# One PSUM bank for three value products and the softmax denominators in a fused attention layer

## The chip, the cores and the metric

The kernel runs on one core of a Trainium2 chip. The metric is the device time of one execution in microseconds (us). A core has a matrix engine (TensorE, in the profile PE for its matrix products and PEld for its weight loads), a vector engine (DVE), a scalar engine for functions and copies (ACT), GpSimd (POOL), and a queue engine that issues transfers (SP). TensorE writes to PSUM alone, which here is used as eight banks of 128 partitions by 512 fp32 numbers.

## The reference

Two layers over 2048 tokens of width 1024. Layer 0 is a gated linear recurrence with a pooling mixer; the change does not touch its arithmetic. Layer 1 is attention with 16 heads of 64 numbers and a cumulative forget bias, cut here to what matters:

```python
q, k, v, g, fl = jnp.split(h @ w_in, ...)
cumf = jnp.cumsum(jax.nn.log_sigmoid(fl + b_f), axis=1)
for blk in range(SEQ // 128):
    logits = q[blk] @ k[:q1].T * scale + cumf[blk][:, None] - cumf[None, :q1]
    probs = softmax(where(mask, logits, -inf), axis=-1)   # exp(...) / sum of exp(...)
    outs.append(probs @ v[:q1])
o = concatenate(outs) * silu(g)
x = x + gate * (o @ w_out)
```

Scores, softmax and values are fp32 in the reference. The kernel keeps that precision by splitting an operand into two parts, `hi` (rounded to the matrix engine's fp32r form) and `lo` (what the rounding left), and adding the products of hi with hi, hi with lo and lo with hi.

## The kernel before

Tokens are worked on in four segments of 512. For each segment layer 0 runs, then layer 1. In layer 1 a head `h` of segment `s` attends to `4*(s+1)` key blocks of 128 keys: those of older segments come back from memory (`K1o`, `K2o`, `Vo`), and the last four are the segment's own (`K1`, `K2`, `Vc`). An own block `b` needs only the queries from `128*b` on, so those four blocks work on 512, 384, 256 and 128 queries. Over the whole program there are 640 key blocks: 448 of 512 queries, and 64 each of 384, 256 and 128.

`attend` (L1116) works on one key block as follows. Two products put the scores, keys by queries, into a bank `pst` (tag `st`, two banks); a block on the diagonal gets a mask by a third. ACT takes the exponential twice, once rounded into `ph` (L1153) and once in place (L1154), and DVE subtracts the two into `pl` (L1156), which ends the bank's use. `values` (L1129) runs two blocks later (`LAG = 2`). It multiplies `ph` with 128 columns that hold the low and the high half of the values, into bank `pov` (tag `o`, one bank, 64 partitions for each half), and `pl` with 66 columns, the high half and two columns of ones, into bank `pol` (tag `o2`, one bank). The sum of `ph` over keys is not taken by TensorE: GpSimd adds every block's `ph` into the tile `la` (L1160 to L1164), 128 partitions by 512, and the sum over the partitions is taken later.

At a head's end ACT copies one half of `pov` (L1175), DVE adds the ones row of `pol` to `la` (L1176) and joins the three parts of the result (L1177, L1178); `la` is then split (L1180, L1181). After every second head, `finish` (L1184) sums `la` over the partitions by four products into `pL`, takes the reciprocal by a logarithm and an exponential, and scales the pair of heads.

While head `h` runs, `max_pass` (L1091) takes the row maxima of head `h+1` in banks `pmx` (DVE reduces them, L1102 and L1104), and writes them, transposed as `pmt`, by an ACT copy into a row of the second query tile (L1114). The second score product of the next head's first block reads that row. `quad_attention` (L1207) steps `attend` and `max_pass` together, and `weave` (L216) deals out between the key blocks the products of projections that later work needs (`pqk`, `pv`, `pgt`, `py`). The tile framework then sets the final order on each engine by its own scheduling, with priorities from the order of the code; each engine works through its list in that order.

Projection weights arrive as `raw`; ACT rounds them (`wt`, L295), and DVE and GpSimd share the subtraction for the low part (L184 by way of L296).

PSUM's eight banks are: `pj` two (projections), `st` two (scores), `o` one, `o2` one, `mx` two (maxima, transposes, `pL`). In layer 0 `o2` also holds one quarter of the output projection (L830).

Of the kernel before, what the change touches and what calls it, by code (L numbers as in the profile page):

```python
# [18 lines left out]
P = 128  # L19
# [16 lines left out]
def trunk(ctx, tc, x, cvec, norm_g, ada_c, ada_w, ada_b, ada_bg, lbp, w0, w0o, w1, w1f, w1o,  # L36
# [31 lines left out]
    def tmp(name, dt=F32, shape=(P, 512)):  # L68
        return tp.tile(list(shape), dt, name=name, tag="tmp")
# [7 lines left out]
    def ps_st(name):  # L77
        return ps.tile([P, 512], F32, name=name, tag="st", bufs=2)

    def ps_o(name):  # L80
        return ps.tile([P, 512], F32, name=name, tag="o", bufs=1)

    def ps_o2(name):
        return ps.tile([P, 512], F32, name=name, tag="o2", bufs=1)

# [3 lines left out]
    def f(ap):  # L89
        return ap.bitcast(F32)  # L90
# [23 lines left out]

    pairr = cp.tile([P, 3 * HD], F32R, name="pairr")
    of = tmp("of")[:, 0:3 * HD]
    V.memset(of, 0.0)
    V.memset(of[:, HD:2 * HD], 1.0)
    V.tensor_copy(pairr, of)

# [699 lines left out]
    def out_first(s):  # L820

        L = seg0[s]
        xs = L["x"] = []
        for tb in range(NTB):
            xt = xp.tile([P, D], F32, name="xo", tag="xs")
            nc.sync.dma_start(xt, x[s * SEG + tb * P:s * SEG + (tb + 1) * P, :])
            xs.append((xt, once([P, 4], f"ss{tb}")))
        wt = next_w(("b", 0))

        L["py"] = wt, [(ps_pj, ps_pj, ps_o2, ps_mx)[tb]("py")[:, 0:256] for tb in range(NTB)]  # L830
        for tb in range(NTB):
            assert L["cores"] >= 3
            proj_N(L["py"][1][tb], wt, L["mix"], tb, (4, 5, 6, 7, 0, 1, 2), last=False)
            yield
# [281 lines left out]
    def attend(s, h):  # L1116
# [5 lines left out]
        vc = L["v", pair]  # L1122
        la = kp.tile([P, SEG], F32, name="la", tag="la", bufs=1)
        po, pol = ps_o("pov"), ps_o2("pol")
        nkb = NTB * (s + 1)
# [3 lines left out]
        def values(b, q0, kb, vv, ph, pl):  # L1129
            end = kb == nkb - 1  # L1130
            mm(po[:, q0:], vv[:, b, 0:P], ph[:, q0:], start=(kb == 0), stop=end)
            mm(pol[0:HD + 2, q0:], vv[:, b, HD:], pl[:, q0:],
               start=(kb == 0), stop=end)

        for c in range(s + 1):
# [8 lines left out]
            for b in range(NTB):  # L1144
# [11 lines left out]
                split_lo(pl[:, q0:], st[:, q0:], ph[:, q0:])  # L1156
                if kb == 0:
                    first = f(ph)
                    if s == 0:
                        G.tensor_copy(la, first)  # L1160
                elif kb == 1 and s > 0:
                    G.tensor_tensor(la, first, f(ph), op=ALU.add)
                else:
                    G.tensor_tensor(la[:, q0:], la[:, q0:], f(ph[:, q0:]), op=ALU.add)  # L1164
                todo.append((b, q0, kb, vv, ph, pl))
# [6 lines left out]
        if j == 0:  # L1172
            L["u", pair] = xp.tile([P, 2, SEG], F32, name="u", tag="xs")
        u = L["u", pair][j * HD:(j + 1) * HD, 0, :]
        S.copy(u, po[HD:P])  # L1175
        V.tensor_tensor(la[0:1], pol[HD:HD + 1], la[0:1], op=ALU.add)  # L1176
        V.tensor_tensor(u, po[0:HD], u, op=ALU.add)  # L1177
        V.tensor_tensor(u, pol[0:HD], u, op=ALU.add)  # L1178
        lh, ll = tmp("lh", F32R), tmp("ll", F32R)
        S.copy(lh, la)  # L1180
        split_lo(ll, la, lh)  # L1181
        L["l", h] = (lh, ll)

    def finish(s, h):  # L1184
# [6 lines left out]
        pL = ps_misc("pL")  # L1191
        for i in range(2):
            for part in range(2):
                mm(pL, pairr[:, (1 - i) * HD:(1 - i) * HD + P], L["l", h - 1 + i][part], start=(i + part == 0), stop=(i + part == 2))
        S.activation(rl, pL, AF.Ln)
# [192 lines left out]
```

## Time and profile before

| | |
|---|---|
| median of 3 runs | 3030.41 us (3029.74 to 3030.75) |
| the profiled execution's own time | 3029.48 us |
| its span, first to last instruction | 3027.8 us |
| mean granted TensorE clock | 0.975 of 2.4 GHz |
| PE busy | 2808.9 us, 93% of the span, 17212 products |
| DVE busy | 2301.3 us, 76% |
| ACT busy | 1826.4 us, 60% |
| POOL busy | 1172.5 us, 39% |

Busy time is the union of an engine's instructions. Products follow one another before the one ahead has ended, and their ends are modelled by the profiler, so PE can show as busy through a short wait; the distance from one start to the next tells what a product costs. The attention of the four segments lies at 382 to 697, 979 to 1388, 1672 to 2164 and 2452 to 3005 us; layer 0 lies between them.

### The profile page before, as it was taken

Reading aid. Unit: us, or ns where it says so; the run is one execution under the profiler, and the core shown is the slowest. Engines: PE = TensorE matmul, PEld = TensorE weight load, DVE = VectorE, ACT = ScalarE, POOL = GpSimd, SP = SyncE. Lnnn points to the kernel's source line nnn. Section 1 sums busy time; section 2 is a strip of 40 time slices with the busy share of each in tenths; the row PEclk is TensorE's granted clock in tenths of the full one; section 3 lists DMA queues with packets and bytes.
Section 4 is the critical chain, followed back from the end, with each engine's and each line's share of the span. In section 5 each row is a group of like instructions: output and inputs, shape, how many; then the busy total and the mean of one; then the engine's idle time right before and its main releaser. Section 6 shows DMA issues by size and latency. Waiting matters only on the chain.

```text
span 3027.8 us, 49244 instructions
## 1 busy us (share of the span) xinstructions
PE 2808.9 (93%) x17212; PEld 2390.2 (79%) x17212; DVE 2301.3 (76%) x4390; ACT 1826.4 (60%) x3743; POOL 1172.5 (39%) x992
## 2 busy tenths in 40 slices
PE   4699999989999999989999999998999999999998
PEld 3688887879888887868878887776898877777777
DVE  8667678776676788886586788889667678888886
ACT  3344566774445666775455676768635467777774
POOL 3111233323211444444212355554432136566665
PEclk9899999999999999999999999999999999999999
DMA  7523365534233444533333443553342334333442
GB/s 246 174 57 102 106 141 139 119 91 124 79 102 110 119 119 104 131 99 115 100 95 116 122 124 115 126 133 113 97 126 71 114 104 115 105 113 107 113 138 86
DMA packets 207888, 348.97 MB, mean 115 GB/s; under 512 B 24068, under 2 KB 70788, under 8 KB 205080
## 3 DMA queue, kind: packets, MB, share of 16 engines
q1 hardware_dynamic: 201816, 329.03, 39.0%
q10 hardware_dynamic: 5824, 16.79, 1.7%
q8 instruction: 137, 2.24, 0.3%
q14 instruction: 111, 0.91, 0.1%
HBM read 293.58 MB, written 52.14 MB: 114 GB/s over the span
## 4 chain that ended last, share of the span: by engine, by line
PE 60%; DVE 19%; ACT 11%; DMA 4%; issue 4%; POOL 1%; SPq 0%; ACTq 0%; DVEq 0%; POOLq 0%
PE py L42 10%; PE pgt L42 8%; PE pqk L42 8%; PE pst L42 6%; PE pv L42 6%; PE pmx L42 4%; PE pov L42 3%; PE pol L42 3%; PE pf L42 3%; PE pq L42 3%; PE pl L42 3%; DVE pl L184 2%; DVE wt L184 2%; ACT wt L295 1%; DMA raw<-in_w_dram 1%
## 5 line engine op out<-in xcount | busy, mean ns | idle before, releaser
L184 POOL TENSOR_TENSOR wt<-raw,wt 128x512 fp32r<-128x512 f32 x287 | 419.5, 1470 | 1030.9 <-ACT wt L295 975.1
L1164 POOL TENSOR_TENSOR la<-la,ph 128x512 f32<-128x512 f32 (+3 forms) x528 | 610.6, 1156 | 385.7 <-ACT ph L1153 342.9
L184 DVE TENSOR_TENSOR pl<-pst,ph 128x512 fp32r<-128x512 f32 (+3 forms) x640 | 386.9, 605 | 133.4 <-ACT pst L1154 102.2
L1153 ACT ACTIVATE ph<-pst 128x512 fp32r<-128x512 f32 (+3 forms) x640 | 340.6, 532 | 235.1 <-PE pst L42 224.9
L42 PE MATMUL pqk<-wt,h 128*128 128x256 f32 x3072 | 433.1, 286 | 5.5 <-DVE h L497 2.7
L42 PEld LDWEIGHTS pqk<-wt,h 128*128 128x128 f32 x3072 | 411.9, 192 | 25.2 <-DVE h L497 3.5
L42 PE MATMUL pgt<-h,wt 128*128 128x512 f32 x1536 | 403.9, 405 | 0.0
L295 ACT CAST wt<-raw 128x512 fp32r<-128x512 f32 x578 | 335.2, 621 | 74.9 <-PE py L42 33.3
L42 PE MATMUL pv<-wt,h 128*128 128x256 f32 x2304 | 345.0, 298 | 10.7 <-DVE h L184 6.6
L42 PEld LDWEIGHTS pv<-wt,h 128*128 128x128 f32 x2304 | 326.1, 204 | 28.9 <-DVE h L184 9.6
L42 PEld LDWEIGHTS pgt<-h,wt 128*128 128x128 f32 x1536 | 293.1, 194 | 63.2 <-issue 1.9
L1154 ACT ACTIVATE pst<-pst 128x512 f32<-128x512 f32 (+3 forms) x640 | 340.0, 531 | 0.0
L184 DVE TENSOR_TENSOR wt<-raw,wt 128x512 fp32r<-128x512 f32 x291 | 265.7, 918 | 73.4 <-ACT wt L295 71.9
L1102 DVE TENSOR_REDUCE mxs<-pmx 128x1 f32<-128x512 f32 x384 | 258.6, 684 | 20.3 <-PE pmx L42 17.2
L42 PE MATMUL py<-wt,o 128*128 128x256 f32 x1536 | 202.2, 286 | 1.4 <-ACT o L1200 1.2
L42 PE MATMUL py<-wt,mix 128*128 128x256 f32 x1536 | 198.2, 287 | 2.3 <-DVE yt L844 2.1
L42 PEld LDWEIGHTS py<-wt,o 128*128 128x128 f32 x1536 | 192.8, 192 | 6.7 <-ACT o L1200 1.5
L42 PEld LDWEIGHTS py<-wt,mix 128*128 128x128 f32 x1536 | 187.9, 191 | 9.8 <-issue 4.5
L42 PE MATMUL pst<-Q,K1o 128*128 128x512 f32 x384 | 162.6, 424 | 23.2 <-DVE pl L184 21.7
L42 PE MATMUL pmx<-K2o,Q 67*128 67x512 f32 x384 | 162.0, 426 | 21.9 <-ACT Q L1077 10.2
L42 PE MATMUL pov<-ph,Vo 128*128 128x512 f32 x384 | 162.8, 425 | 6.6 <-ACT ph L1153 6.2
L1104 DVE CUSTOM_DVE_ANT_0 pmx<-pmx,mq 128x128 f32<-128x128 f32 (+3 forms) x256 | 124.6, 497 | 55.6 <-PE pmx L42 53.8
(251 smaller groups left out, 5309.1 us busy)
## 6 DMA issues: line engine op xcount, KB each, us to landing
raw<-in_w_dram SPq DMA_DIRECT2D x448, 256.0 KB, 3.5
K2o<-k2d SPq DMA_DIRECT2D x192, 160.0 KB, 3.4
Vo<-vd SPq DMA_DIRECT2D x96, 260.0 KB, 2.7
K1o<-k1d SPq DMA_DIRECT2D x96, 256.0 KB, 3.4
raw<-in_w1o_dram SPq DMA_DIRECT2D x66, 256.0 KB, 3.6
raw<-in_w0o_dram SPq DMA_DIRECT2D x64, 256.0 KB, 3.2
vd<-Vc SPq DMA_DIRECT2D x48, 260.0 KB, 8.1
ada<-in_ada_w_dram ACTq DMA_DIRECT2D x12, 1024.0 KB, 5.0
```

The costliest lines, as they stand in the source:

```text
L42: return nc.tensor.matmul(*a, **k)
L184: (eng or V).tensor_tensor(out_t, full, f(hi), op=ALU.subtract)
L295: S.copy(wt[:, 0, sl, :], raw)
L1102: V.tensor_reduce(mxs[:, i, c:c + 1], pm[:, 0:n], axis=AX.X, op=ALU.max)
L1104: V.tensor_tensor_reduce(pm[:, 0:n], pm[:, 0:n], mq[:, SEG - n:], 1.0, NEG, op0=ALU.add, op1=ALU.max, accum_out=mxs[:, i, c:c + 1])
L1153: S.activation(ph[:, q0:], st[:, q0:], AF.Exp)
L1154: S.activation(st[:, q0:], st[:, q0:], AF.Exp)
L1164: G.tensor_tensor(la[:, q0:], la[:, q0:], f(ph[:, q0:]), op=ALU.add)
```

## The change

The three partial products of a key block all go into the one bank `pov`, one after the other: `ph` with the 66 columns of high values and ones (64 value rows and the rows of ones), `ph` with the 64 columns of low values, `pl` with the 66 columns. Row 64 of the bank then holds the whole denominator. GpSimd's sum `la` and the bank `pol` go. The bank set free is given to the scores, which now have three. At a head's end ACT rounds row 64 into a row of a new constant tile `sums` (zero elsewhere), copies the 64 result rows to `u`, and DVE writes the low part of the denominator 32 partitions further. `finish` then needs one product over 97 partitions in place of four over 128. The quarter of the output projection that was in `o2` takes a score bank.

```diff
@@ -75,13 +75,10 @@
         return ps.tile([P, 512], F32, name=name, tag="pj", bufs=2)
 
     def ps_st(name):
-        return ps.tile([P, 512], F32, name=name, tag="st", bufs=2)
+        return ps.tile([P, 512], F32, name=name, tag="st", bufs=3)
 
     def ps_o(name):
         return ps.tile([P, 512], F32, name=name, tag="o", bufs=1)
-
-    def ps_o2(name):
-        return ps.tile([P, 512], F32, name=name, tag="o2", bufs=1)
 
     def ps_mx(name):
         return ps.tile([P, 512], F32, name=name, tag="mx", bufs=2)
@@ -112,11 +109,15 @@
     eps1 = cp.tile([P, 1], F32, name="eps1")
     V.memset(eps1, EPS)
 
-    pairr = cp.tile([P, 3 * HD], F32R, name="pairr")
-    of = tmp("of")[:, 0:3 * HD]
+    pairr = cp.tile([P, P], F32R, name="pairr")
+    of = tmp("of")
     V.memset(of, 0.0)
-    V.memset(of[:, HD:2 * HD], 1.0)
-    V.tensor_copy(pairr, of)
+
+    sums = cp.tile([P, SEG], F32R, name="sums")
+    V.tensor_copy(sums, of)
+    V.memset(of[0:HD, 0:HD], 1.0)
+    V.memset(of[HD:P, HD:P], 1.0)
+    V.tensor_copy(pairr, of[:, 0:P])
 
     NL = 7
     lmask = cp.tile([P, NL, P // 2], U8, name="lmask")
@@ -827,7 +828,7 @@
             xs.append((xt, once([P, 4], f"ss{tb}")))
         wt = next_w(("b", 0))
 
-        L["py"] = wt, [(ps_pj, ps_pj, ps_o2, ps_mx)[tb]("py")[:, 0:256] for tb in range(NTB)]
+        L["py"] = wt, [(ps_pj, ps_pj, ps_st, ps_mx)[tb]("py")[:, 0:256] for tb in range(NTB)]
         for tb in range(NTB):
             assert L["cores"] >= 3
             proj_N(L["py"][1][tb], wt, L["mix"], tb, (4, 5, 6, 7, 0, 1, 2), last=False)
@@ -1120,17 +1121,16 @@
         Q1, Q3, K1, K2 = L["ops", h]
         pair, j = h // 2, h % 2
         vc = L["v", pair]
-        la = kp.tile([P, SEG], F32, name="la", tag="la", bufs=1)
-        po, pol = ps_o("pov"), ps_o2("pol")
+        po = ps_o("pov")
         nkb = NTB * (s + 1)
         kb = 0
         todo = []
 
         def values(b, q0, kb, vv, ph, pl):
             end = kb == nkb - 1
-            mm(po[:, q0:], vv[:, b, 0:P], ph[:, q0:], start=(kb == 0), stop=end)
-            mm(pol[0:HD + 2, q0:], vv[:, b, HD:], pl[:, q0:],
-               start=(kb == 0), stop=end)
+            mm(po[0:HD + 2, q0:], vv[:, b, HD:], ph[:, q0:], start=(kb == 0), stop=False)
+            mm(po[0:HD, q0:], vv[:, b, 0:HD], ph[:, q0:], start=False, stop=False)
+            mm(po[0:HD + 2, q0:], vv[:, b, HD:], pl[:, q0:], start=False, stop=end)
 
         for c in range(s + 1):
             if c < s:
@@ -1154,14 +1154,6 @@
                 S.activation(st[:, q0:], st[:, q0:], AF.Exp)
                 pl = tmp("pl", F32R)
                 split_lo(pl[:, q0:], st[:, q0:], ph[:, q0:])
-                if kb == 0:
-                    first = f(ph)
-                    if s == 0:
-                        G.tensor_copy(la, first)
-                elif kb == 1 and s > 0:
-                    G.tensor_tensor(la, first, f(ph), op=ALU.add)
-                else:
-                    G.tensor_tensor(la[:, q0:], la[:, q0:], f(ph[:, q0:]), op=ALU.add)
                 todo.append((b, q0, kb, vv, ph, pl))
                 if len(todo) > LAG:
                     values(*todo.pop(0))
@@ -1171,15 +1163,11 @@
             values(*t)
         if j == 0:
             L["u", pair] = xp.tile([P, 2, SEG], F32, name="u", tag="xs")
-        u = L["u", pair][j * HD:(j + 1) * HD, 0, :]
-        S.copy(u, po[HD:P])
-        V.tensor_tensor(la[0:1], pol[HD:HD + 1], la[0:1], op=ALU.add)
-        V.tensor_tensor(u, po[0:HD], u, op=ALU.add)
-        V.tensor_tensor(u, pol[0:HD], u, op=ALU.add)
-        lh, ll = tmp("lh", F32R), tmp("ll", F32R)
-        S.copy(lh, la)
-        split_lo(ll, la, lh)
-        L["l", h] = (lh, ll)
+        r = j * HD
+        hi = sums[r:r + 1]
+        S.copy(hi, po[HD:HD + 1])
+        S.copy(L["u", pair][r:r + HD, 0, :], po[0:HD])
+        split_lo(sums[r + 32:r + 33], po[HD:HD + 1], hi)
 
     def finish(s, h):
 
@@ -1189,9 +1177,7 @@
             return
         u, rl = L["u", pair][:, 0, :], L["u", pair][:, 1, :]
         pL = ps_misc("pL")
-        for i in range(2):
-            for part in range(2):
-                mm(pL, pairr[:, (1 - i) * HD:(1 - i) * HD + P], L["l", h - 1 + i][part], start=(i + part == 0), stop=(i + part == 2))
+        mm(pL, pairr[0:97], sums[0:97], start=True, stop=True)
         S.activation(rl, pL, AF.Ln)
         S.activation(rl, rl, AF.Exp, scale=-1.0)
         mix = L["mix"]
```

How the instructions stand on TensorE in the middle of a head, in the third segment while `pv` is dealt out. Before:

```order
L42 MATMUL pst<-Q_20978,K1o 128x512
L42 MATMUL pst<-Q_20979,K2o 128x512
L42 MATMUL pol<-pl,Vo 66x512
L42 MATMUL pmx<-K2o,Q_21326 128x512
L42 MATMUL pov<-ph,Vo 128x512
L42 MATMUL pmx<-K2o,Q_21326 128x512
```

The same place in the changed kernel, where the value products have 66, 64 and 66 columns:

```order
L42 MATMUL pst<-Q_20659,K1o 128x512
L42 MATMUL pst<-Q_20660,K2o 128x512
L42 MATMUL pov<-ph,Vo 66x512
L42 MATMUL pov<-ph,Vo 64x512
L42 MATMUL pov<-pl,Vo 66x512
L42 MATMUL pmx<-K2o,Q_21001 128x512
```

A key block carries three value products instead of two, all to one bank.

TensorE where the 12th head of the third segment ends and the next begins (`pmt` are the transposed maxima of the next head, `pqkT` the transposes for the head after). Before:

```order
L42 MATMUL pol<-pl,Vc 66x256
L45 MATMUL pmt<-ident,m 1x128
L45 MATMUL pqkT<-ident,qk 128x128 x2
L42 MATMUL pov<-ph,Vc 128x128
L45 MATMUL pqkT<-ident,qk 128x128 x2
L42 MATMUL pol<-pl,Vc 66x128
L42 MATMUL pst<-Q_21325,K1o 128x512
L42 MATMUL pst<-Q_21326,K2o 128x512
L42 MATMUL pst<-Q_21325,K1o 128x512
L42 MATMUL pst<-Q_21326,K2o 128x512
L42 MATMUL pqk<-wt,h_17222 128x256 x14
```

And in the changed kernel:

```order
L42 MATMUL pov<-pl,Vc 66x256
L42 MATMUL pov<-ph,Vc 66x128
L42 MATMUL pov<-ph,Vc 64x128
L42 MATMUL pov<-pl,Vc 66x128
L45 MATMUL pmt<-ident,m 1x128 x4
L45 MATMUL pqkT<-ident,qk 128x128 x4
L42 MATMUL pst<-Q_21000,K1o 128x512 x3
L42 MATMUL pqk<-wt,h_16969 128x256 x4
L42 MATMUL pst<-Q_21001,K2o 128x512 x3
L42 MATMUL pqk<-wt,h_16969 128x256 x8
```

The next head starts with three blocks of scores instead of two, and the transposes stand behind the old head's last value product.

ACT where the fifth head of the third segment ends; `Q<-pmt` writes the maxima row of the next head. Before:

```order
L1153 ACTIVATE ph<-pst 128x128
L1154 ACTIVATE pst<-pst 128x128
L1114 ACTIVATE Q_19237<-pmt 1x512
L1175 COPY u<-pov 64x512
L1073 ACTIVATE Q_19568<-pqkT,c_qkg 64x512
```

And in the changed kernel:

```order
L1153 ACTIVATE ph<-pst 128x128
L1154 ACTIVATE pst<-pst 128x128
L1080 DMA Q_19280<-q4d 16x512
L1081 DMA K_19282<-cfd 16x512
L1168 CAST sums<-pov 1x512
L1169 COPY u<-pov 64x512
L1115 ACTIVATE Q_18957<-pmt 1x512
L1074 ACTIVATE Q_19279<-pqkT,c_qkg 64x512
```

The row of maxima that the next head waits for now stands behind the two reads of the finished bank. In the changed kernel's list this is so for about three heads in four; before, it stood first or behind the copy of `u` alone.

## Rows read from the trace of the kernel before

**Rows 1.** The page: busy time of TensorE, and the chain that ended last.

```profile
PE 2808.9 (93%) x17212; PEld 2390.2 (79%) x17212; DVE 2301.3 (76%) x4390; ACT 1826.4 (60%) x3743; POOL 1172.5 (39%) x992
...
PE 60%; DVE 19%; ACT 11%; DMA 4%; issue 4%; POOL 1%; SPq 0%; ACTq 0%; DVEq 0%; POOLq 0%
PE py L42 10%; PE pgt L42 8%; PE pqk L42 8%; PE pst L42 6%; PE pv L42 6%; PE pmx L42 4%; PE pov L42 3%; PE pol L42 3%; PE pf L42 3%; PE pq L42 3%; PE pl L42 3%; DVE pl L184 2%; DVE wt L184 2%; ACT wt L295 1%; DMA raw<-in_w_dram 1%
```

**Rows 2.** Busy time by stretch, the last segment's attention: engine busy us (instructions).

```profile
2452.00:3005.00 553.00, 527.26 (x2933) 420.25 (x2934) 466.78 (x835) 397.04 (x785) 342.59 (x277) 1.00 0.39 110
```

**Rows 3.** Timeline of TensorE inside a head: start us, us, what.

```profile
2513.51 0.39 PE L42 MATMUL pst<-Q,K1o 128*128 128x512 f32 x1
...
2513.98 0.39 PE L42 MATMUL pol<-pl,Vo 128*66 128x512 f32 x1
2514.21 0.39 PE L42 MATMUL pov<-ph,Vo 128*128 128x512 f32 x1
...
2514.67 0.40 PE L42 MATMUL pqk<-wt,h 128*128 128x256 f32 x2
```

**Rows 4.** Timeline of TensorE on the diagonal, products of 384 and 128 queries.

```profile
2503.97 0.34 PE L42 MATMUL pov<-ph,Vc 128*128 128x384 f32 x1
2504.15 0.75 PE L42 MATMUL pqk<-wt,h 128*128 128x256 f32 x5
...
2505.94 0.27 PE L42 MATMUL pov<-ph,Vc 128*128 128x128 f32 x1
2506.05 0.27 PE L45 MATMUL pmt<-ident,m 128*1 128x128 f32 x1
```

**Rows 5.** Timeline of TensorE around products of 48 columns (the forget gates).

```profile
2432.80 4.72 PE L42 MATMUL pqk<-wt,h 128*128 128x256 f32 x38
2437.36 3.86 PE L42 MATMUL pfl<-h,wf 128*48 128x512 f32 x16
2441.06 2.20 PE L42 MATMUL pv<-wt,h 128*128 128x256 f32 x17
```

**Rows 6.** Groups of instructions that go or shrink: busy us, mean ns, idle before.

```profile
L1164 POOL TENSOR_TENSOR la<-la,ph 128x512 f32<-128x512 f32 (+3 forms) x528 | 610.6, 1156 | 385.7 <-ACT ph L1153 342.9
...
L184 DVE TENSOR_TENSOR ll<-la,lh 128x512 fp32r<-128x512 f32 x64 | 44.0, 687 | 2.7 <-ACT lh L1180 1.4
L1176 DVE TENSOR_TENSOR la<-pol,la 1x512 f32<-1x512 f32 x64 | 43.8, 685 | 41.0 <-PE pol L42 29.9 <-POOL la L1164 9.9 <-PE pqkT L45 0.5
L1177 DVE TENSOR_TENSOR u<-pov,u 64x512 f32<-64x512 f32 x64 | 43.7, 682 | 6.8 <-ACT u L1175 5.0
L42 PE MATMUL pL<-lh,pairr 128*128 128x512 f32 x64 | 27.2, 426 | 1.5 <-DVE mxs L1102 1.5
```

**Rows 7.** Who waited for the score tile and its parts: us, times.

```profile
  PEld pst L42: 59.4, 78
  PE pst L42: 35.1, 31
  PEld pov L42: 26.3, 73
  PEld pol L42: 17.6, 41
```

**Rows 8.** DVE's weight splits: mean in the page, then shortest/median/longest ns.

```profile
L184 DVE TENSOR_TENSOR wt<-raw,wt 128x512 fp32r<-128x512 f32 x291 | 265.7, 918 | 73.4 <-ACT wt L295 71.9
...
L184 DVE TENSOR_TENSOR wt<-raw,wt x291: 668/693/2193, 104.1 to 3000.1; 128x512 fp32r<-128x512 f32 x146
```

**Rows 9.** Timeline of ACT at a head's end.

```profile
2506.25 0.58 ACT L1175 COPY u<-pov 64x512 f32<-64x512 f32 x1 [0.25 <-PE pov L42]
...
2506.86 0.58 ACT L1114 ACTIVATE Q<-pmt 1x512 fp32r<-1x512 f32 x1
```

**Rows 10.** Timeline at the end of the last segment's attention.

```profile
3007.63 0.27 PE L42 MATMUL pol<-pl,Vc 128*66 128x128 f32 x1
...
3010.15 0.50 PE L42 MATMUL pL<-lh,pairr 128*128 128x512 f32 x1
```

## The prediction

> **What bounds the kernel now.** I read the page first. TensorE is busy 93% of the span, DVE 76%, and the chain that ended last is TensorE for 60%, DVE for 19%, ACT for 11% [rows 1]. So TensorE is the bound most of the time, but not all of it: for four tenths of the span the end was set by something that TensorE waited for. The change sits in attention, so I asked for busy time by stretch; in the last segment TensorE is busy 527 of 553 us and DVE 467 [rows 2]. Since neighbouring products overlap in such rows, the timeline is the better witness of what a product costs. Inside a head five 512-query products start at 2513.51 and the next follows at 2514.67 [rows 3]: 1.16 us for five, 0.232 us each, back to back without a hole, though each row says 0.39. A product of 66 columns (`pol`, 2513.98 to 2514.21) takes the same place as one of 128. In such stretches TensorE has no room, and a further product moves everything behind it. The holes lie elsewhere; the waits for the score tile show which of them the change can reach [rows 7].
>
> **Added products.** Each of 640 key blocks gets one product more. For 448 of them it is 448 x 0.232 = 103.9 us. On the diagonal one of 384 queries takes 0.18 us (2503.97 to 2504.15) and one of 128 takes 0.11 [rows 4]; one of 256 takes 0.12 (38 products between 2432.80 and 2437.36) [rows 5]. That is 64 x 0.41 = 26.2 us, together 130.1 us of TensorE time.
>
> The new product of low values has 64 columns and stands between two of 66. A cost for changing the width used would appear where widths change now: sixteen products of 48 columns stand between products of 128, at 2437.36 and 2441.06, and take 3.70 us, 0.231 each, with the neighbours undisturbed [rows 5]. So I add nothing for the width. The Trainium skill speaks against the change here: TensorEngine Tiling (Array Packing), section Tiling Modes, says in its list of key properties that switching the tiling mode drains TensorE. This trace does not agree for 48 columns, if those run as a narrower tile; by the rule the sum would be that of the drain rival below.
>
> **Removed products.** `finish` issues 128 products into `pL` and will issue 32; 96 x 0.232 = 22.3 us go. They are 512 queries wide like the others [rows 6], and the row count does not enter. Net on TensorE: +107.8 us. If all of it lands and nothing else changes, the time is 3137.
>
> **The third score bank.** A score bank is held from the first product until DVE's subtraction. TensorE's wait for it is 35.1 us in 31 cases if only time past a product's modelled end is counted, and 59.4 us in 78 cases by the weight loads, which stand ahead of the products [rows 7]. The mean is 47. A third bank lets TensorE run one block further ahead, 553/256 = 2.2 us in the last segment [rows 2], which covers nearly every such wait. I take -40; bounds 0 and -59.
>
> **Waits for the exponential and the subtraction.** The value products wait for `ph` and `pl`: 26.3 and 17.6 us by the weight loads [rows 7], 44 at most. With three products where two stood, more time passes between a block's scores and its use, and the scores run further ahead. I take a third, -14; bounds 0 and -44.
>
> **DVE and GpSimd.** At a head's end four DVE instructions of 0.685 us become one [rows 6]: 64 x 2.06 = 132 us. ACT loses a cast of `la` and gains one of a row. GpSimd loses 528 additions, 611 us [rows 6], and a few more that start the sums. Its own time is on the chain for 1% [rows 1]. But DVE's weight splits, two inputs from SBUF, have a median of 693 ns, a mean of 918 and a longest of 2193 [rows 8]. If half the excess, (918 - 693) x 291 = 65 us, is GpSimd's doing and half its work goes, another 16 us of DVE return.
>
> So DVE loses 148 of 2301 us. It is 19% of the chain, 575 us; in proportion 37 us of chain would go. About half of that is the bank waits already counted, so I take -20; bounds 0 and -37.
>
> **The head's end.** Here something is added. ACT's row cast and copy of the finished bank now stand ahead of the row of maxima that the next head's scores need, and both wait for the last product of `pl`. An ACT instruction on one row costs 0.58 us, as much as the copy [rows 9]. From the last value product, 0.27 us [rows 10], to the row are thus 0.27 + 3 x 0.58 = 2.0 us and the hops between engines. What covers it on TensorE, in the order shown, are four transposes (0.11 each, as the one-column product in [rows 4]), one to three score products and 4 to 12 projection products: 0.44 + 3 x 0.232 + 4 x 0.12 = 1.6 us where the first form stands. Some heads fall short by 0.4 us and others by none; if the cover were gone, the whole cast would show, 64 x 0.58 = 37 us. I take +15; bounds 0 and 37. Queued behind those ACT instructions are the next exponentials, so a late row also delays the new head's first value products.
>
> **The segment's end.** From the last product to the first of `pL` are 2.5 us, through DVE, ACT and their hops [rows 10]. Now it is the product's 0.27, a row cast of 0.58 and a split of 0.69 with two hops, about 1.7. Four times 0.8 is -3.
>
> The constant tile and the layer-0 quarter in a score bank cost nothing: the first is one instruction beside the first loads, and in layer 0 two score banks are left, as many as before.
>
> **The sum.** 107.8 - 40 - 14 - 20 + 15 - 3 = +46. Against the profiled execution's own time, 3029.5, that is 3075. (The median of the runs, 3030.4, is 0.9 above it, the span 1.7 below.)
>
> A second count goes by the chain. The present value products hold 3% and 3% of it [rows 1], about 180 us, out of twice 130 us issued: 69% of such a product's time reaches the end. Then the new ones add 90, the `pL` products take away 15, half of POOL's 1% goes (15) and half of the 2% that the `pl` subtraction holds (30): +30, which gives 3059. The first count may miss relief that has no wait of its own; the second cannot see where the chain moves to. I take the middle, **3067 us**, 1.2% slower.
>
> **Rivals.**
> *Faster, because DVE and the score banks are the real limit.* The place is the score bank's round from product to exponentials to subtraction. All bounds together return 59 + 44 + 37 + 3 = 143 us, with no cost at the head's end: 3029.5 + 107.8 - 143 = 2994; half way there from the break-even, 3012. It decides from the point where more than 108 us return, three quarters of everything that can. For it speak the 19% of DVE; against it the dense stretches of [rows 3], where no wait is left to return. Chance 0.10.
> *No visible change or nearly none*, 3020 to 3042: the chain's count is right and the third bank gives its full 59 us, 3030. Chance 0.13.
> *Nothing returns.* The waits were at other places by chance of the order, and move on: 3029.5 + 107.8 = 3137, with the head's end 3152; anything above 3100. Chance 0.13.
> *The drain.* If the 64-column product empties the array before and after itself, each switch costs the part of a product that now overlaps its neighbour, 0.39 - 0.232 = 0.16 us: 2 x 640 x 0.16 = 205 us on top, 3272. [Rows 5] speak against it. Chance 0.03.
> *The forecast*, 3042 to 3100: chance 0.61.
>
> **How the numbers follow.** This kernel's runs agree closely; about 0.2%, 6 us, is what a measurement can tell from no change. The range 3026 to 3122 leaves out about a tenth on either side: the faster case below, the drain and the upper half of "nothing returns" above. For the forecast alone it is 3042 to 3100. Faster by over 0.2%, below 3024: 0.11, the faster case and a little of the next. Within 0.2%: 0.09. Slower: 0.80.
>
> **What would show it.** In the changed profile TensorE's products number 544 more, each new one 0.23 us from start to start inside a head; if the 64-column product is followed at 0.3 us or more, the drain is real. The score products' wait for the subtraction falls from 35 and 59 us to under 12 and 20. POOL's busy time falls by more than 611 us, and DVE's by about 150. At a head's end the second score product waits for the row of maxima by some tenths of a us. The last segment's attention, 553 us, grows by 25 to 35 us; the first, with only own blocks, hardly changes. The prediction is wrong if TensorE's starts are already sparse where the value products stand, or if the wait for scores moves to another bank, `pov` above all, which now has three products to end before ACT and DVE read it.

## The result and the profile after

The changed kernel takes 3070.59 us (median of 4 runs, 3066.98 to 3073.14) where the kernel before takes 3030.58 (3029.74 to 3039.66): a ratio of 1.0124, 95% interval 1.0102 to 1.0147, so 1.2% slower. The forecast of 3067 us holds in size. The experiments below show that two of its terms were wrong by much, in opposite directions, which the time alone could not tell.

The page of the profiled execution after (its own time 3073.14 us, span 3071.4) answers to the first row of [rows 1]:

```profile
PE 2870.6 (93%) x17756; PEld 2420.0 (79%) x17756; DVE 2086.5 (68%) x4200; ACT 1820.6 (59%) x3743; POOL 488.1 (16%) x400
```

There are 544 products more, 640 new ones less 96 into `pL`. GpSimd lost 684 us of busy time. DVE lost 215 where the forecast had 148; the 67 us between will matter.

The busy time by stretch, first and last segment's attention, cut at the start and end of attention as [rows 2]; the columns are the stretch, its length, then PE, PEld, DVE, ACT and POOL busy with counts, granted clock, DMA share, GB/s:

```profile
385.00:708.00 323.00, 297.02 (x1938) 256.88 (x1936) 200.50 (x439) 215.68 (x453) 48.45 (x40) 0.97 0.46 116
...
2462.00:3046.00 584.00, 557.68 (x3139) 435.65 (x3140) 414.48 (x788) 394.32 (x784) 51.02 (x40) 0.99 0.36 105
```

The last segment grew from 553 to 584 us, as forecast; the first grew by 8 us, from 315. DVE fell from 467 to 414 us in a stretch that became longer.

The timeline of TensorE at a head's diagonal shows what the three products cost, start and duration in us:

```profile
2516.54 0.66 PE L42 MATMUL pov<-ph,Vc 128*66 128x512 f32 x2
2517.04 0.39 PE L42 MATMUL pov<-pl,Vc 128*66 128x512 f32 x1
2517.27 0.33 PE L42 MATMUL pst<-Q,K 128*128 128x128 f32 x2
```

The first row is the product of 66 columns and the one of 64. Three products take 0.73 us from start to start, 0.24 each, where those of [rows 3] took 0.232. A drain around the 64-column product, as the prediction priced it, would show here as 0.16 us on either side of it. There is none. It holds for the whole trace: where a product of 512 queries and 66 columns stands ahead of the one of 64, the median from start to start is 0.237 us against older keys and 0.262 against own ones, and from the one of 64 to the next of 66 it is 0.231 and 0.233.

The Trainium skill says that changing the tiling mode drains TensorE (TensorEngine Tiling (Array Packing), section Tiling Modes). If the 64-column product runs as a narrower tile, which the profile does not show, these rows do not agree with it, as [rows 5] did not.

What TensorE waited for on the score and value tiles (by products, PE, and by the weight loads ahead of them, PEld: us in total, times, longest) answers to [rows 7]:

```profile
PEld pst L42 <- DMA K2o<-k2d: 41.3, 36, 2.8
...
PE pst L42 <- DMA K2o<-k2d: 29.3, 26, 2.5
...
PEld pov L42 <- DVE pl L185: 26.7, 61, 3.8
...
PEld pov L42 <- ACT ph L1153: 20.7, 26, 4.5
PEld pst L42 <- ACT Q L1115: 20.3, 32, 2.8
...
PE pov L42 <- ACT ph L1153: 14.0, 13, 4.3
...
PE pov L42 <- DVE pl L185: 10.5, 19, 3.6
...
PE pst L42 <- ACT Q L1115: 9.7, 12, 2.4
```

The old wait of a score product for the subtraction, 35.1 by the products and 59.4 by the weight loads, has gone from the list. In its place stands a wait of 29.3 and 41.3 us for the second key tile of older segments, `K2o`, which comes back from memory. Before, the same wait was small:

```profile
PEld pst L42 <- DMA K2o<-k2d: 3.3, 7, 1.3
...
PE pst L42 <- DMA K2o<-k2d: 1.2, 2, 1.0
```

The timeline of the changed kernel shows one of its waits (SPq is SP's queue, which issues the transfer):

```profile
2565.10 0.85 SPq L1089 DMA_DIRECT2D K2o<-k2d  x2
...
2567.25 0.40 PE L42 MATMUL pst<-Q,K1o 128*128 128x512 f32 x1
2568.84 0.50 PE L42 MATMUL pst<-Q,K2o 67*128 67x512 f32 x1 [1.20 <-DMA K2o<-k2d]
```

The first of the two transfers is issued 3.7 us before the product starts, and 3.7 us is the median from issue to landing of a `K2o` transfer in this trace, so the product stands ready and waits. `K2o` has three buffers (L1088, `bufs=3`), which `attend` and `max_pass` share. In the last segment, with 16 heads, this wait occurs 19 times by the products, 21.1 of the 29.3 us.

### The profile page after: what moved, and what is told of

Its sections match the earlier page's. It is cut to its first block, busy times and chain, and to the rows that moved or that the text cites. A ratio compares the mean times of both kernels' runs of the same rounds, so it can differ in the third digit from the quotient of the medians.

```text
span 3071.4 us, 48673 instructions
## 1 busy us (share of the span) xinstructions
PE 2870.6 (93%) x17756; PEld 2420.0 (79%) x17756; DVE 2086.5 (68%) x4200; ACT 1820.6 (59%) x3743; POOL 488.1 (16%) x400
## 5 line engine op out<-in xcount | busy, mean ns | idle before, releaser
L185 POOL TENSOR_TENSOR wt<-raw,wt 128x512 fp32r<-128x512 f32 x287 | 410.0, 1436 | 2211.0 <-ACT wt L296 1886.8
L42 PE MATMUL pqk<-wt,h 128*128 128x256 f32 x3072 | 421.9, 286 | 5.2 <-DVE h L498 2.6
L42 PEld LDWEIGHTS pqk<-wt,h 128*128 128x128 f32 x3072 | 404.8, 193 | 20.0 <-DVE h L498 3.4
L42 PE MATMUL pgt<-h,wt 128*128 128x512 f32 x1536 | 394.8, 401 | 0.0
L42 PE MATMUL pv<-wt,h 128*128 128x256 f32 x2304 | 329.8, 292 | 5.9 <-DVE h L185 3.1
L42 PEld LDWEIGHTS pv<-wt,h 128*128 128x128 f32 x2304 | 311.9, 198 | 21.4 <-DVE h L185 6.6
L185 DVE TENSOR_TENSOR wt<-raw,wt 128x512 fp32r<-128x512 f32 x291 | 258.1, 890 | 93.2 <-ACT wt L296 91.6
L42 PE MATMUL pov<-ph,Vo 128*66 128x512 f32 (+1 forms) x768 | 252.2, 405 | 9.6 <-ACT ph L1153 9.5
L42 PE MATMUL pst<-Q,K2o 67*128 67x512 f32 x384 | 158.8, 419 | 33.3 <-DMA K2o<-k2d 29.3
L591 ACT ACTIVATE Dt<-Dt 128x512 f32<-128x512 f32 x112 | 70.0, 630 | 152.4 <-DVE Dt L590 150.8
```

Of the source, the lines that this page charges most:

```text
L42: return nc.tensor.matmul(*a, **k)
L185: (eng or V).tensor_tensor(out_t, full, f(hi), op=ALU.subtract)
L591: S.activation(Dt, Dt, AF.Exp)
```

## The experiments

All times are medians, and each ratio is to the kernel before run beside it, with its 95% interval. "Two banks" are score banks; work tiles are the buffers of the pool `tp`. The edits are shown without the lines around them. A ratio is good to 3 to 7 us, a difference of two ratios to 6 to 10 us.

| kernel | us (lowest to highest) | ratio | interval |
|---|---|---|---|
| changed, one buffer more for `K2o` | 3022.29 (3021.33 to 3023.44) | 0.9965 | 0.9953 to 0.9976 |
| changed, eight work tiles (control) | 3060.10 (3057.01 to 3061.28) | 1.0088 | 1.0075 to 1.0101 |
| changed, two banks (nine work tiles) | 3043.97 (3039.68 to 3057.80) | 1.0040 | 1.0025 to 1.0056 |
| changed, two banks, `K2o` four | 3032.43 (3027.14 to 3041.74) | 0.9998 | 0.9986 to 1.0009 |
| before, `K2o` four | 3033.60 (3023.22 to 3041.15) | 0.9997 | 0.9984 to 1.0010 |
| changed, no product of low values | 2944.88 (2941.56 to 2960.62) | 0.9725 | 0.9701 to 0.9749 |
| before, one more product a block | 3151.66 (3143.16 to 3154.99) | 1.0383 | 1.0363 to 1.0402 |
| before, no additions on GpSimd | 2960.54 (2954.59 to 2965.35) | 0.9754 | 0.9733 to 0.9775 |
| before, fills for the additions | 2969.53 (2966.64 to 2973.68) | 0.9801 | 0.9784 to 0.9818 |
| before, touch and fills | 2977.58 (2970.08 to 2982.14) | 0.9823 | 0.9803 to 0.9843 |
| before, additions that read only `la` | 3091.17 (3086.31 to 3098.59) | 1.0203 | 1.0181 to 1.0225 |
| changed, additions put back | 3126.80 (3126.26 to 3132.93) | 1.0323 | 1.0306 to 1.0341 |

### Is the new wait the buffers of K2o?

A fourth buffer for `K2o` needs room, so the pool of work tiles has eight buffers in place of nine. The control has the eight alone.

```diff
-    tp = E(tc.tile_pool(name="tp", bufs=9))
+    tp = E(tc.tile_pool(name="tp", bufs=8))
-        K2 = kp.tile([P, SEG], F32R, name="K2o", tag="k2o", bufs=3)
+        K2 = kp.tile([P, SEG], F32R, name="K2o", tag="k2o", bufs=4)
```

> The changed kernel with a fourth buffer for the older keys' second tile (K2o), which pays for its place with one temporary buffer (eight, not nine). In the changed kernel the score products wait 29 us (past modelled ends) to 41 us (by weight loads) for K2o transfers, where the kernel before waited 1 to 3 us. Theory A (the change removed the bank wait and ran into the K2o buffers behind it): that wait falls under 8 us and the time to 3032 to 3048 us. Rival B (the K2o rows are a symptom: transfers are late because their issue is late, and a buffer more only moves the wait to another operand): 3060 us or more.

> The changed kernel with eight temporary buffers instead of nine and nothing else, the control for the run before. Two temporaries per head went with the row sums, so both theories expect no difference, 3064 to 3077 us; if it is slower than that, its distance is to be added to what the fourth K2o buffer gave.

The control's waits for `K2o`:

```profile
PEld pst L42 <- DMA K2o<-k2d: 35.6, 35, 2.6
...
PE pst L42 <- DMA K2o<-k2d: 23.5, 30, 2.3
```

With four buffers the wait of score products for `K2o` is absent from both lists, and the kernel takes 3022 us: 38 us less than its control, and 0.35% less than the kernel before, with an interval that excludes no change. This version is faster than both kernels, and by more than theory A gave (3032 to 3048). The control itself ran 11 us below the changed kernel, and below its expected range, though the order of instructions on TensorE is the same row for row. Its granted clock was higher, 0.980 against 0.977 in the profiled executions; the clock not granted is 3057.9 x 0.020 = 61 us there and 3071.4 x 0.023 = 71 us in the changed kernel, so by this estimate up to 10 of the 11 us are the clock's. Whether that comes from the ninth tile or from runs made apart stays open; so numbers below are taken against the kernel that ran beside them where there is one.

### What is the third bank worth?

```diff
-        return ps.tile([P, 512], F32, name=name, tag="st", bufs=3)
+        return ps.tile([P, 512], F32, name=name, tag="st", bufs=2)
```

The first kernel has this edit alone. The second has the four `K2o` buffers and eight work tiles as well. The third gives the kernel before the four buffers and eight tiles.

> The changed kernel with two score banks; the third stands unused. Theory A (the third bank gave back 35 to 59 us of bank wait, and its running ahead created the K2o wait): the score products wait for DVE's subtraction again, 25 to 50 us, the K2o wait falls under 10 us, and the time is 3075 to 3100 us. Rival B (TensorE's added work alone covers the old bank wait, the third bank gives nothing): 3064 to 3077 us, with hardly any wait for the subtraction.

> The changed kernel with two score banks, four K2o buffers and eight temporary buffers: the same as the 3022 us version but for the third bank. Theory A (with transfers no longer late, the third bank is worth the bank wait that is left with two banks, 2 us past modelled ends and 20 by the weight loads): 3028 to 3042 us. Rival (the third bank is worth nothing even then; the whole gain is the K2o buffer's): 3016 to 3027 us.

> The kernel before with a fourth K2o buffer and eight temporary buffers. Theory A (the K2o wait came with the change; before it is 1 to 3 us): no difference, 3026 to 3040 us, or slower if the ninth temporary buffer was needed there. Rival (the fourth buffer helps any version, by other transfers that wait behind the K2o issue on the same queue): 3015 us or less, and then the best version of the change would not beat it.

With two banks the changed kernel is faster: 3044 us, 16 less than the control with three (which ran beside it, but has one work tile less), and 25 less than the changed kernel by the ratios (1.0124 - 1.0040 = 0.84%; the same tiles, but runs made apart). Both expected ranges were missed, 3075 to 3100 and 3064 to 3077. With four `K2o` buffers it is the other way: two banks 3032, three banks 3022, so the third bank is worth 10 us (0.9998 - 0.9965 = 0.33%). The kernel before gains nothing from the fourth buffer (3034). The waits with two banks and three buffers show the exchange:

```profile
PEld pst L42 <- DVE pl L185: 20.5, 68, 0.6
...
PEld pst L42 <- DMA K2o<-k2d: 14.8, 18, 2.0
...
PE pst L42 <- DMA K2o<-k2d: 8.6, 11, 1.6
...
PE pst L42 <- DVE pl L185: 2.2, 2, 2.1
```

Without any third bank the wait for the subtraction has fallen to 2.2 and 20.5 us, from 35.1 and 59.4 [rows 7]. So most of the old bank wait left for another reason than the bank, and what the bank could still return was small. What it did bring was 15 us more of wait for `K2o` by the products and 21 by the weight loads (control against two banks). The third bank also changes the order that the scheduler gives TensorE (in the traces about one row in seven stands elsewhere), so this is the effect of that bank with its order, not of a bank alone.

### Do the added products land in full?

The first kernel is the changed one without the product of `ph` with the low values (so the low parts of the values are missing from the result); the second is the kernel before, with one more product of 66 columns for each block, into `pol` (which then also holds sums that are counted twice).

```diff
-            mm(po[0:HD, q0:], vv[:, b, 0:HD], ph[:, q0:], start=False, stop=False)
```

```diff
+            mm(pol[0:HD + 2, q0:], vv[:, b, HD:], ph[:, q0:], start=(kb == 0), stop=False)
             mm(pol[0:HD + 2, q0:], vv[:, b, HD:], pl[:, q0:],
-               start=(kb == 0), stop=end)
+               start=False, stop=end)
```

> The changed kernel without the product of the probabilities with the low half of the values (this term of the result is left out), so two value products per key block as before, all else as in the change. 130 us of TensorE time go. Theory A (TensorE is the bound where the value products stand): 110 to 130 us return, 2940 to 2960 us. Rival B (by the chain, two thirds of a value product reach the end): about 90 us, 2975 to 2990 us. Rival C (the waits for K2o, the row of maxima and the exponentials become the limit at once): less than 60 us, over 3010 us.

> The kernel before with one product more per key block, of the probabilities with the 66 columns, added into the second bank (the denominators then count a term twice, so the output is not the reference's). It adds 130 us of TensorE time and leaves GpSimd's row sums, the head's end and two score banks as they were. If an added product lands in full whatever stands around it: 3145 to 3165 us. If the added time alone covers most of the bank wait (the wait for the subtraction falls from 59 us by the weight loads to about 20, as with two banks in the changed kernel): 3090 to 3125 us, and the rest of what the change gave back is the row sums' and the head's end. If it covers all that the change gave back: under 3080 us.

Taking the product away returns 121 us (1.0124 - 0.9725 = 3.99% of 3030); adding one costs 116 us (3.83%). The forecast had 130. So about nine tenths of a TensorE product in attention reach the end, in either kernel. In both, the scheduler also moved other products (a quarter to nearly half of TensorE's rows stand elsewhere), so neither figure is that of a product alone; that two different orders give nearly the same speaks for it. The second count by the chain, at 69%, was too low. In the kernel before with the added product the bank wait stays:

```profile
PE pst L42 <- DVE pl L184: 33.6, 29, 2.4
```

It was 35.1 us [rows 7], so more TensorE work does not cover it.

### What were the additions on GpSimd worth?

GpSimd's additions go, and one fill for each head stands in their place (the denominators lack the sum of `ph`; so they do in the next kernels on the kernel before).

```diff
-                    G.tensor_tensor(la[:, q0:], la[:, q0:], f(ph[:, q0:]), op=ALU.add)
+                    G.memset(la, 1.0)
```

> The kernel before without GpSimd's 576 additions over key blocks; a memset of the sum tile per head stands for them, so the denominators are not summed. Everything else stays, DVE's and ACT's work at the head's end too. By the prediction's term for GpSimd (16 us of DVE time, half of it felt): 3020 to 3035 us. Rival: the additions hold up the head's end or the weight splits more than the waits show, and their absence gives 25 us or more, under 3008 us.

The time falls by 75 us (2.46%), as the rival had it and not the prediction's term, though TensorE issues the same products in nearly the same order (about a dozen of some 5200 rows stand elsewhere). The page, and the waits for the subtraction:

```profile
PE 2782.1 (94%) x17212; PEld 2377.3 (80%) x17212; DVE 2215.8 (75%) x4390; ACT 1822.9 (62%) x3743; POOL 522.7 (18%) x464
```

```profile
PEld pst L42 <- DVE pl L184: 16.8, 47, 1.2
...
PE pst L42 <- DVE pl L184: 4.4, 8, 0.8
```

DVE executes the same 4390 instructions in 85 us less, and the bank wait falls to 4.4 and 16.8 us with two banks. This is where most of the bank wait came from.

The bank wait gives 31 us of the 75 by the products and 43 by the weight loads. Another part is TensorE's clock. The second segment's attention with the additions, and the same stretch without them (columns as above):

```profile
979.00:1388.00 409.00, 378.93 (x2256) 315.68 (x2255) 322.49 (x610) 282.48 (x583) 172.69 (x148) 0.97 0.44 112
```

```profile
979.00:1388.00 409.00, 388.90 (x2371) 325.38 (x2370) 309.12 (x627) 295.04 (x608) 59.30 (x57) 1.00 0.44 117
```

With the additions TensorE is idle longer, and its mean granted clock is 0.97, a mix of 2.4 and 1.2 GHz; without them it is 1.00. Over the whole execution the clock not granted is 3027.8 x 0.025 = 76 us before and 2960.6 x 0.021 = 62 us without: by this estimate up to 14 us. The rest of the 75 us is not traced to one wait.

Most of the instructions that became shorter are not those the prediction looked at. In the kernel before two groups of DVE read (busy us, mean ns):

```profile
L1199 DVE TENSOR_TENSOR u<-u,sg 128x512 f32<-128x512 f32 x32 | 37.1, 1161 | 0.1
L171 DVE TENSOR_TENSOR t_qk<-r_qk 128x16 f32<-128x16 f32 x32 | 27.2, 850 | 1.6 <-ACT r_qk L169 1.4
```

Both have two SBUF inputs. Without the additions they take 716 and 500 ns, while the weight splits fall from 918 to 872 only:

```profile
L1193 DVE TENSOR_TENSOR u<-u,sg 128x512 f32<-128x512 f32 x32 | 22.9, 716 | 0.1
...
L171 DVE TENSOR_TENSOR t_qk<-r_qk 128x16 f32<-128x16 f32 x32 | 16.0, 500 | 1.7 <-ACT r_qk L169 1.5
```

Three things go with the additions: GpSimd's occupation, its reading of SBUF, and its hold on the buffers of `ph`. Three more kernels part them; in each, one more fill stands at a head's first block. The first puts two fills of the same columns where an addition stood: GpSimd is nearly as busy, but reads nothing and needs no `ph`. The second copies two columns of `ph` ahead of the two fills: it waits for `ph` and holds its buffer, but reads next to nothing. The third doubles `la`: it reads two SBUF inputs, but not `ph`.

```diff
-                    G.tensor_tensor(la[:, q0:], la[:, q0:], f(ph[:, q0:]), op=ALU.add)
+                    G.memset(la[:, q0:], 1.0)
+                    G.memset(la[:, q0:], 1.0)
```

```diff
-                    G.tensor_tensor(la[:, q0:], la[:, q0:], f(ph[:, q0:]), op=ALU.add)
+                    G.tensor_copy(la[:, q0:q0 + 2], f(ph[:, q0:q0 + 2]))
+                    G.memset(la[:, q0:], 1.0)
+                    G.memset(la[:, q0:], 1.0)
```

```diff
-                    G.tensor_tensor(la[:, q0:], la[:, q0:], f(ph[:, q0:]), op=ALU.add)
+                    G.tensor_tensor(la[:, q0:], la[:, q0:], la[:, q0:], op=ALU.add)
```

> The kernel before, with each of GpSimd's additions replaced by two constant fills of the same columns (so the denominators lack their high part): GpSimd stays busy for about as long, but reads nothing from SBUF. Theory (GpSimd's reading of SBUF holds up DVE's instructions with two SBUF inputs, and those hold the score banks): nearly the whole gain of the kernel without additions (2961 us) stays, 2955 to 2985 us, and TensorE's wait for the subtraction stays under 10 and 25 us, against 35 and 59. Rival (GpSimd's own queue, its late share of the weight splits, counts): 3015 to 3040 us, and the wait stays at 25 to 35 and 45 to 60 us. In between, both count, in proportion.

> The kernel before, with each of GpSimd's additions replaced by a copy of two columns of the exponentials and two constant fills (the denominators lack their high part): GpSimd waits for the exponentials and holds their buffers as before, and is busy for about as long, but reads next to nothing. Theory (reading beside DVE): 2960 to 2985 us, as with constant fills alone (2970). Rival (the buffers): 3010 to 3040 us.

> The kernel before, with each of GpSimd's additions replaced by one that doubles the tile of sums (the denominators lack their high part): GpSimd still reads two SBUF inputs for as long, but no longer reads the exponentials, so it holds none of their buffers. Theory (GpSimd's reading of SBUF beside DVE's): the time stays near that of before, 3010 to 3040 us. Rival (the additions held the buffers of the exponentials and came late in that way): it falls to 2960 to 2985 us, as with constant fills. In between, both count.

With the fills the time is 60 us below the kernel before, with touch and fills 54. The pages of the three, in this order:

```profile
PE 2779.2 (94%) x17212; PEld 2375.1 (80%) x17212; DVE 2220.1 (75%) x4390; ACT 1823.5 (62%) x3743; POOL 1044.4 (35%) x1616
```

```profile
PE 2788.4 (94%) x17212; PEld 2382.6 (80%) x17212; DVE 2217.6 (74%) x4390; ACT 1822.3 (61%) x3743; POOL 1187.6 (40%) x2192
```

```profile
PE 2826.2 (92%) x17212; PEld 2403.5 (78%) x17212; DVE 2299.3 (75%) x4390; ACT 1825.5 (59%) x3743; POOL 1076.6 (35%) x1040
```

DVE's busy time is the cleanest reading. With GpSimd as busy as before (1044 and 1188 us, against 1172) but hardly reading, the same DVE instructions take 2220 and 2218 us, 81 and 84 less than before. With GpSimd reading other data than `ph` they take 2299, as before (2301). So it is the reading that lengthens them, and neither GpSimd's being busy nor its hold on `ph`; that an addition may differ from a fill in more than its inputs is not parted here. Occupation and the hold on `ph` together account for what is left between no additions and touch with fills, 17 us by the medians, 21 by the ratios. The groups in the kernel with fills show it by instruction, and that GpSimd was at work:

```profile
L1159 POOL MEMSET la<- 128x512 f32 (+3 forms) x576 | 263.4, 457 | 30.7
...
L1196 DVE TENSOR_TENSOR u<-u,sg 128x512 f32<-128x512 f32 x32 | 23.0, 718 | 0.1
```

The 718 ns stand against 1161. The Trainium skill has this as a rule (SBUF — State Buffer, section Who interferes with whom): a VectorE instruction with two SBUF inputs contends with a GpSimd instruction that reads SBUF, and not with one that only writes it. DVE's busy time agrees: where GpSimd fills and does not read, it is 81 us less, nearly the 85 us of no additions at all.

The time of the third kernel is a miss upwards: expected near 3030, measured 3091. Besides the bank wait, which stays (32.3 and 53.0 us), it has another:

```profile
PEld pst L42 <- DMA K2o<-k2d: 40.1, 19, 9.4
...
PE pst L42 <- DMA K2o<-k2d: 33.6, 15, 9.1
```

```profile
SPq L290 <- POOL wt L184: 565.1, 239, 16.9
```

The second fence is a wait of SP's queue: it stands 565 us (423 before) behind GpSimd's weight splits, and the `K2o` transfers are issued in that queue; why it stands there longer is not shown. The waits for `K2o` are 34 to 40 us, where they were 1 to 3. Two more things differ: a wait of layer 0's products `pl` for the tile `Dt` is 27.5 us where it was 14.0, and the granted clock is 0.964 where it was 0.975, by 111 less 76 us of clock not granted an estimate of up to 35 us. Together these are more than the 63 us above before; how they share them stays open. What this run says for the question is only that the reading keeps DVE as slow as it was and that the time does not fall.

Last, the changed kernel (with eight work tiles) with the additions put back, their result unused:

```diff
+        la = kp.tile([P, SEG], F32, name="la", tag="la", bufs=1)
+                if kb == 0:
+                    G.tensor_copy(la, f(ph))
+                else:
+                    G.tensor_tensor(la[:, q0:], la[:, q0:], f(ph[:, q0:]), op=ALU.add)
```

> The changed kernel with eight work tiles in place of nine (3060 us measured so, from 3057 to 3061), and GpSimd's row sums put back, whose result nobody reads. Theory (the additions alone cost the kernel before 75 us, and their going is the change's largest relief): 3110 to 3140 us, DVE's busy time grows by 60 to 100 us over 2086 us, and TensorE waits for the subtraction again, 10 us or more. Rival (with three score banks the additions are covered, and the relief belongs to the banks): at most 3075 us.

It takes 3127 us, as the theory had it: 67 more than the control's 3060 (71 by the ratios), with TensorE's order nearly the same (six of some 5500 rows stand elsewhere). The page and the waits for the subtraction:

```profile
PE 2887.4 (92%) x17756; PEld 2420.7 (77%) x17756; DVE 2175.4 (69%) x4200; ACT 1823.8 (58%) x3743; POOL 1204.8 (38%) x1040
```

```profile
PEld pov L42 <- DVE pl L185: 70.4, 100, 3.9
...
PE pov L42 <- DVE pl L185: 38.8, 52, 3.7
```

DVE is 84 us busier than in the control (2091.4). With three banks its lateness no longer shows at the score bank: it shows at the value product, 38.8 us where the control has 12.2:

```profile
PE pov L42 <- DVE pl L185: 12.2, 21, 3.5
```

So a third bank alone does not cover a late DVE; it moves the wait to `pov`.

## Why the prediction was right, and where it was not

The direction was right for the reason given: TensorE has hardly any room in attention, and the added products are the largest term. The size was right by luck, as the terms show.

**The products.** Right in kind: 130.1 forecast, 116 and 121 measured by adding and by taking one, no cost for the width. The going of the `pL` products (-22.3) was not tried by itself.

**The third bank, -40.** This step failed. By the runs it costs 16 (control) to 25 us as the change has it, and returns 10 with a fourth `K2o` buffer. The prediction read the right wait in [rows 7], and the wait did go, but for the larger part with GpSimd's additions (35.1 to 4.4 us when they alone go). And running further ahead was priced as free: by the trace its cost is that the next `K2o` is waited for. The prediction asked "what is late next" of the exponentials and not of the transfers, though `K2o` stood among TensorE's waits with 3.3 us already.

**DVE and GpSimd, -20.** This step failed the other way: the additions alone are worth 67 to 75 us. The rows it used were sound: the weight splits return 13.5 us of DVE without additions, and 16 were forecast. But [rows 8] show one form among many, and other forms returned the remaining 72, most of them with two SBUF inputs. (Some 15 us of it are two small forms with one tensor input; they do not follow the reading clearly, since one of them keeps 14.4 of its 16.0 us with fills and 8.2 with touch and fills.) Then DVE's time was priced at its 19% share of the chain. 85 us of DVE came back and the kernel fell by 75: DVE held the score bank that TensorE waited for, which is 31 to 43 us of it, and TensorE's clock rose with fewer waits, up to 14. The bounds given, 0 and -37, did not hold it.

**DVE's busy time after.** The 215 us that DVE lost are the 132 of the head's end, as forecast, and 81 to 85 from GpSimd's reading, where 16 were forecast.

**The head's end, +15.** Too large. The wait of the score products for the row of maxima rose from 6.4 to 9.7 us by the products and from 15.1 to 20.3 by the weight loads: 3 to 5 us. What a late row does to the exponentials behind it was not tried.

**The segment's end, -3.** Smaller. The timeline at the end of the last segment's attention:

```profile
3049.59 0.28 PE L42 MATMUL pov<-pl,Vc 128*66 128x128 f32 x1
...
3049.70 2.24 PE L42 MATMUL py<-wt,o 128*128 128x256 f32 x17
3049.91 0.58 ACT L1168 CAST sums<-pov 1x512 fp32r<-1x512 f32 x1 [0.69 <-PE pov L42]
3050.50 0.58 ACT L1169 COPY u<-pov 64x512 f32<-64x512 f32 x1
3051.11 0.69 DVE L185 TENSOR_TENSOR sums<-pov,sums 1x512 fp32r<-1x512 f32 x1 [1.57 <-ACT u L1169]
3051.85 0.50 PE L42 MATMUL pL<-sums,pairr 97*128 97x512 f32 x1
```

From product to `pL` are 2.26 us where 1.7 were forecast and 2.52 were before [rows 10]. The split of the row starts only after the copy of `u`, which the forecast had beside it. Nor is this TensorE's loss here: between the two it works on 17 products of `py`, and before it had 18 of them in the same place, so what the segment's end was worth cannot be read from this distance alone.

**The waits for the exponential and the subtraction, -14.** For `ph` they fell from 26.3 to 20.7 us by the weight loads; for `pl` they rose from 17.6 to 26.7. Together they did not fall (43.9 to 47.4), so this term was about nothing.

**The sum again.** 119 for the products (between 116 and 121), -71 for the additions (between 67 and 75), 25 for the third bank, and -22 for `pL` taken over from the forecast: 51. The measured difference is 40 (3070.6 less 3030.6). The 11 between are the head's-end DVE work, the other small terms and what the parts do to one another, by difference and not tried, and not far beyond what such differences are good to. The first count had 107.8 - 40 - 20 = 48 for the same four, so it came out near by an exchange: it credited the bank with 65 us too much and the additions with 51 too little (more, since its 20 were to cover the head's-end DVE work as well), and the products cost 11 less. The 3067 of the forecast is the middle between that count, 3075, and the one by the chain, 3059, which had the products 26 to 31 us too cheap and neither the bank's cost nor the additions' worth; that the middle lies within 4 us of the measured time is luck.

What the prediction named as its danger, a wait that moves to another bank, came about in another place: it moved to a transfer. And its 6 us for what can be told from no change came from three runs; later executions of the kernel before lie between 3022 and 3040 us.

## What to carry to other kernels

Before GpSimd is given work "beside" the others, look at all of DVE's two-input forms and not at the largest group, and look whether DVE holds something that the bound engine waits for: here additions of 611 us on GpSimd [rows 6] and a few more cost 81 to 85 us of DVE and 67 to 75 us of the kernel. What these forms take over their shortest is a bound and not the answer: in the kernel before it adds up to some 210 us over the `tensor_tensor` instructions without a PSUM input, and only part of it went with the additions. The kernel without the work tells which part. When a bank is added so that an engine may run ahead, look at the buffers of everything else that this engine reads there; one more of them turned +16 to +25 us into -10. And a sum that comes out right does not show that its terms are; parts undone one by one do.

## What was not expected of the hardware

GpSimd's reading lengthens very small DVE instructions too: the one of 128x16 with two inputs took 850 ns with the additions and 500 without. Fills of the same columns leave DVE's busy time within 5 us of no additions at all (2220 and 2216 us), though they keep GpSimd nearly as busy (1044 us against 1172).
